# Per-token factors spread over channels by transposes, and values transposed two chunks at a time

## The chip, the cores and the metric

One Trainium2 chip, one of its cores. The metric is device microseconds of one execution of the whole program, as the median of runs on the chip. Beside the runs stands one profiled execution, whose trace is read below.

## The reference

One inference step of a one-layer hybrid decoder: 512 prompt tokens and 8 x 8 sampled tokens, 576 in all, with 1024 channels. Cut to what matters here:

```python
u = rmsnorm(h, norm_mix)                       # h * rsqrt(mean(h*h) + eps) * g, per token
proj = u @ w_in                                # z, xbc, dt, rw
# group A: SSD (Mamba-2) with conv, silu, gate, and a grouped RMSNorm of the output
yg = yg * lax.rsqrt(jnp.mean(yg * yg, axis=-1, keepdims=True) + NORM_EPS)   # 2 groups of 512 channels
# group B: RWKV-7, 16 heads of 64 channels
kk = heads(k * k_k)
kk = kk / jnp.maximum(jnp.sqrt(jnp.sum(kk * kk, axis=-1, keepdims=True)), 1e-12)   # per token and head
s = s * w - (s @ kk) (kk * a)^T + v k^T        # per token; evaluated here in chunks of 64 tokens
o = s @ r
on = (o - mean(o)) * lax.rsqrt(var(o) + GN_EPS) * ln_x_w + ln_x_b           # per token and head
out = concat(y_ssd, (on + bonus) * gate) @ w_out
h += out; h += SwiGLU(rmsnorm(h)); h += sigmoid(rmsnorm(h) @ w_plg) * (p @ w_plp); y = rmsnorm(h)
```

Four kinds of factor belong to a token (or to a token and a head) and are applied to all its channels: the row norms, the group norm of group A, the norm of `kk`, and the deviation of `o`.

## The kernel before, in words

Activations are kept with channels on the 128 partitions and the 576 tokens along the free dimension (64 sampled tokens first, then 512 of the prompt). A linear layer multiplies f32 data as high and low parts, three matmuls of 128x128 by 128x288 each (`mm3`, L210 to L212), into a tile of the pool `lin`: two tiles of two PSUM banks each, used in turn by all projections, by the low-rank products (`lora`), the gate products and the bonus sums (`fsum`, L225). The other four banks are `cx` (two), `tr` (one) and `cb` (one).

Group B runs in four quarters of four heads, that is two channel tiles (`jj`) each. For a quarter, `prep` makes the decays, keys and norms, `gram` the products between tokens of a chunk, `solve` and `combine` invert the triangular blocks (VectorE, with round trips through DRAM; L638 and L640 are its inner loop), `chain` walks through the 9 chunks of 64 tokens (chunk 0 is the sampled tokens), and `head_norm` normalises the output. Projections that are not needed yet are put in between (`fill`). The program text gives priorities; a planner in the framework puts the instructions of each engine in order ahead of time, from its own costs, so parts of different quarters are interleaved finely on every engine. Semaphores and the reuse of tiles follow from that order. `head_norm` of the last quarter has a raised priority.

A factor per token is made with the tokens on the partitions and must come back to channels on the partitions. Tokens are cut in five windows of 128, `WIN`; 576 is four and a half times 128, so the fifth overlaps the fourth by 64.

- `token_sums` (L469) adds up squares over the channels of a head: matmuls whose output has tokens on partitions.
- `inv_norm` takes the square root (ScalarE) and the reciprocal (VectorE).
- `by_channel` copies the factor to 64 columns a head (L486, or L490 and L492) and multiplies each window by the identity, as a plain f32 product (L495), into one PSUM bank of 512 tokens; the last 64 tokens go by a product over 64 partitions (L498) into a second bank. It hands the two pieces back one after the other, and VectorE multiplies each into `kk` (L548, bank `cb`) or into the output (L877, banks `cx`).
- `rstd_by_token` does the same for the factors of a whole token (sums L306, products L313). It is called for the first norm, twice for the group norm of group A, for the two norms around the feed-forward part, and for the two halves of the final norm.

In `chain`, the values `v` of a chunk are needed with tokens on partitions, in the tile `suv(g)`, where each of the two heads of a channel tile sits on its own half of the partitions. `vwin(w)` transposes 128 tokens from token 64 w on (two transposes, L722, into `tr`), and `vput` copies from it with ScalarE: one half to chunk w + 1 for the first head, the other to chunk w for the second head. The first chunk's and the last chunk's other heads come from small 64x64 products with the identity (`edge`, L811 and L812), the last one by way of the tile `vl`. So each chunk is preceded by a window of its own:

```python
        for g in range(1, 9):
            if g < 8:
                w = vwin(g)
                vput(g + 1, 0, w)
                vput(g, 1, w)
```

`bktok` transposes the keys of a chunk (L730, also into `tr`), and `core`, `prompt_state` and `outp` are the products of the chunk.

Of the kernel before, what the change touches and what calls it, by code (L numbers as in the profile page):

```python
# [74 lines left out]
def hybrid_step(ctx, tc, A):  # L75
# [31 lines left out]
    WIN = ((0, 0, 128), (1, 128, 128), (2, 256, 128), (3, 384, 128), (4, 448, 128))  # L107
# [140 lines left out]
    def tr_ps():  # L248
        return bank(sq_, "tr", 1)
# [49 lines left out]
    def rstd_by_token(acc, scale, a=0, b=NT, banks=None):  # L299

        t = None if banks else lin_bank()
        n = (b - a) // P
        ws = [(a + i * P, 0) for i in range(n)] + [(b - P, 64)] * ((b - a) % P // 64)
        st = banks[1][:, 96:96 + len(ws)] if banks else t[:, 600:600 + len(ws)]
        for i, (c, _) in enumerate(ws):
            T.matmul(st[:, i:i + 1], acc[:, c:c + P], ones[:, 0:1], start=True, stop=True)  # L306
        rn = cp.tile([P, 5], F32, tag="rn5", name=nm("rn5"), bufs=2)
        act(rn[:, 0:len(ws)], st, AF.Sqrt, scale=scale, bias=eps_t[:, 0:1])
        V.reciprocal(rn[:, 0:len(ws)], rn[:, 0:len(ws)])
        for i, (c, p) in enumerate(ws):  # L310
            o = c + p - a
            o = banks[o // 512][:, o % 512:o % 512 + P - p] if banks else t[:, o:o + P - p]
            T.matmul(o, rn[p:P, i:i + 1].to_broadcast([P - p, P]), ident[p:P, p:P],  # L313
                     start=True, stop=True)
        return None if banks else t[:, 0:b - a]
# [3 lines left out]
    act(r0[:, 0:512], banks[0][:])  # L319
    act(r0[:, 512:NT], banks[1][:, 0:64])  # L320
# [145 lines left out]
    def token_sums(st, jj, sq):  # L466

        for w, a, n in WIN:
            T.matmul(st[:, w * 4 + jj * 2:w * 4 + jj * 2 + 2], sq[:, a:a + n], blk[:, 0:P:64], start=True, stop=True)  # L469
# [11 lines left out]
    def by_channel(rn, jj, psum, tag):  # L481

        rnv = rn[:].rearrange("p (w h) -> p w h", w=5)[:, :, jj * 2:jj * 2 + 2].unsqueeze(3)
        if tag:
            rx = sp.tile([P, 5, 2, 64], F32, tag=tag, name=nm(tag), bufs=1)
            V.tensor_copy(rx[:], rnv.to_broadcast([P, 5, 2, 64]))  # L486
            rx4 = rx[:, 4]
        else:
            rx = slot("rx", [P, 4, 2, 64])
            V.tensor_copy(rx[:], rnv[:, 0:4].to_broadcast([P, 4, 2, 64]))  # L490
            rx4 = s2.tile([P, 2, 64], F32, tag="rx4", name=nm("rx4"))
            V.tensor_copy(rx4[:], rnv[:, 4].to_broadcast([P, 2, 64]))  # L492
        ps = psum()
        for w, a, n in WIN[:4]:
            T.matmul(ps[:, a:a + n], rx[:, w].rearrange("p a b -> p (a b)"), ident[:], start=True, stop=True)  # L495
        yield 0, 512, ps[:, 0:512]
        ps = psum()
        T.matmul(ps[:, 0:64], rx4[64:128].rearrange("p a b -> p (a b)"), ident[64:128, 64:128], start=True, stop=True)  # L498
        yield 512, NT, ps[:, 0:64]

    def prep(s):
# [26 lines left out]
        for jj in jj2:  # L528
# [18 lines left out]
            for a0, b0, ps in by_channel(rn, jj, cb_ps, ""):  # L547
                V.scalar_tensor_tensor(kk[:, a0:b0], k[:, a0:b0], par("k_k", j), ps, ALU.mult, ALU.mult)  # L548
# [155 lines left out]
    def chain(s):  # L704
# [9 lines left out]
        def vput(g, e, ps):  # L714
            h = H[1 - e]
            src = ps[h].rearrange("p (j c) -> p j c", j=2)[:, :, e * 64:e * 64 + 64]
            act(suv(g)[h, :, :, e], src.unsqueeze(2).to_broadcast([64, 2, 2, 64]))

        def vwin(w):
            ps = tr_ps()  # L720
            for jj in jj2:
                T.transpose(ps[:, jj * P:(jj + 1) * P], vv[jj][:, w * 64:w * 64 + 128], ident[:])  # L722
            return ps[:, 0:256]
# [85 lines left out]
        edge = tr_ps()  # L809
        for jj in jj2:  # L810
            T.matmul(edge[H[1], jj * P:jj * P + 64], vv[jj][H[0], 0:64], ident[H[0], 0:64], start=True, stop=True)  # L811
            T.matmul(edge[H[0], jj * P + 64:jj * P + 128], vv[jj][H[1], 512:576], ident[H[1], 64:128],  # L812
                     start=True, stop=True)
        vlast = sp.tile([64, 2, 64], F32, tag="vl", name=nm("vl"))
        act(vlast[:], edge[0:64, 0:256].rearrange("p (j c) -> p j c", j=2)[:, :, 64:128])
        for e in range(2):
            G.memset(suv(1)[H[e], :, 0, e], 0.0)
        vput(0, 0, edge[:, 0:256])
        w = vwin(0)
        vput(1, 0, w)  # L820
        vput(0, 1, w)
        for e in range(2):
            G.tensor_copy(suv(0)[H[e], :, 0, e], ident[H[e], H[e]].unsqueeze(1).to_broadcast([64, 2, 64]))
        for g in range(1, 9):
            if g < 8:
                w = vwin(g)
                vput(g + 1, 0, w)
                vput(g, 1, w)
            else:
                act(suv(8)[0:64, :, :, 1], vlast[:].unsqueeze(2).to_broadcast([64, 2, 2, 64]))  # L830
            bktok(g)
            core(g)
            prompt_state(g)
# [19 lines left out]
    def head_norm(s, ahead=()):  # L853
# [18 lines left out]
        for jj in jj2:  # L872
# [3 lines left out]
            for a, b, ps in by_channel(rn, jj, cx_ps, "rxg"):  # L876
                V.scalar_tensor_tensor(o[:, a:b], o[:, a:b], par("ln_x_w", j), ps, ALU.mult, ALU.mult)  # L877
# [80 lines left out]
    def ssd():  # L958
# [193 lines left out]
        def gated(g):  # L1152
# [18 lines left out]
            act(std[:, 0:512], banks[0][:])  # L1171
            act(std[:, 512:NT], banks[1][:, 0:64])
# [314 lines left out]
```

## Time and profile before

| | |
|---|---|
| Median of 3 runs | 1425.92 us (1424.22 to 1428.69) |
| Profiled execution | 1428.9 us, span 1427.1 us |
| Mean granted TensorE clock in it | 0.944 |
| Busy: TensorE / VectorE / ScalarE / GpSimd | 1318.6 / 726.2 / 584.3 / 548.9 us |
| TensorE matmul records | 10007 |
| DMA | 135.48 MB, mean 95 GB/s |

In the rows of the profile, PE is TensorE's matmul, PEld its weight load, DVE VectorE, ACT ScalarE, POOL GpSimd, SP the queue that issues DMAs. A group's row gives line, engine, operation, output tile <- input tiles, shapes and count, then busy time in us and the mean duration in ns, then the idle time of the engine just before and what ended it. A row of the time order gives start, length (first start to last end of the merged instructions), engine and instruction; matmuls overlap, so the distance between starts tells how long TensorE is held. A row of the chain gives start, the length that the chain spends there, and the place. A row of the waits gives who waited for whom, the us in total, how often, and the longest.

From about 900 us on, the span is the feed-forward part and what follows it, with TensorE busy almost without a gap; before that, the four quarters (to about 725 us) and group A's scan (to about 870 us) share the engines.

### The profile page before, as it was taken

The page shows a single profiled execution, that of the slowest core. Times are in us where ns is not written, and L with a number is a line of the kernel's source. Part 1 is how long each engine was busy: PE and PEld are TensorE (multiplying, and loading weights), DVE is VectorE, ACT ScalarE, POOL GpSimd, SP SyncE. Part 2 cuts the span into 40 slices and gives each one's busy share as a digit, 9 for nine tenths or more (in the row PEclk, how much of TensorE's full clock was granted, in tenths as well). Part 3 has the DMA queues.
Part 4 walks back from the last instruction along what each step waited for, and adds up shares of the span by engine and source line. Part 5 has one row for each costly group of instructions (what it writes and reads, how often), then busy time and mean ns, then how long its engine had stood idle before and what let it go on. Part 6 is the DMA issues. An engine that isn't in the chain of part 4 may idle for free.

```text
span 1427.1 us, 25249 instructions
## 1 busy us (share of the span) xinstructions
PE 1318.6 (92%) x10007; PEld 1215.1 (85%) x10007; DVE 726.2 (51%) x1338; ACT 584.3 (41%) x1185; POOL 548.9 (38%) x545
## 2 busy tenths in 40 slices
PE   6897999999989988979889998999999999999996
PEld 6786897798779967957766787999999999999986
DVE  6548768696767657854365564522222122122264
ACT  6564436543653355434422254433232332222252
POOL 5344515622434235214354454522232332344432
PEclk9998999999989989969959999999999999999998
DMA  4322233233223312343513541322322222223421
GB/s 155 126 60 75 72 107 107 60 89 109 63 86 87 101 56 86 114 135 116 181 61 127 167 123 45 90 74 84 86 82 82 82 82 82 84 83 82 146 80 67
DMA packets 94453, 135.48 MB, mean 95 GB/s; under 512 B 34704, under 2 KB 39056, under 8 KB 94336
## 3 DMA queue, kind: packets, MB, share of 16 engines
q1 hardware_dynamic: 94336, 133.88, 30.7%
q8 instruction: 78, 1.28, 0.4%
q14 instruction: 39, 0.32, 0.1%
HBM read 106.10 MB, written 27.75 MB: 94 GB/s over the span
## 4 chain that ended last, share of the span: by engine, by line
PE 67%; DVE 18%; ACT 4%; DMA 4%; issue 3%; POOL 1%; SPq 1%; DVEq 0%; ACTq 0%; POOLq 0%
PE lin L210 17%; PE lin L212 17%; PE lin L211 17%; DVE Tt L640 2%; DVE tmp L638 2%; PE lin L580 2%; DVE h L369 2%; PE d L1116 1%; PE y L1147 1%; DVE wlo L195 1%; PE y L1149 1%; DMA L<-Ld 1%; DMA raw<-wts 1%; PE cx L802 1%; DVE suv L785 1%
## 5 line engine op out<-in xcount | busy, mean ns | idle before, releaser
L210 PE MATMUL lin<-xhi,whi 128*128 128x288 f32 (+1 forms) x1488 | 450.8, 303 | 4.5 <-ACT xhi L92 1.9
L212 PE MATMUL lin<-xhi,wlo 128*128 128x288 f32 (+1 forms) x1488 | 449.9, 302 | 3.3 <-DVE wlo L195 1.9
L211 PE MATMUL lin<-xlo,whi 128*128 128x288 f32 (+1 forms) x1488 | 449.2, 302 | 0.6 <-POOL xlo L183 0.6
L195 POOL TENSOR_TENSOR wlo<-raw,whi 128x512 fp32r<-128x512 f32 x137 | 180.6, 1319 | 467.0 <-ACT whi L92 452.6
L92 ACT ACTIVATE whi<-raw 128x512 fp32r<-128x512 f32 (+1 forms) x272 | 169.0, 621 | 403.1 <-PE lin L211 330.6
L210 PEld LDWEIGHTS lin<-xhi,whi 128*128 128x128 f32 (+1 forms) x1488 | 283.7, 191 | 13.3 <-issue 5.1
L212 PEld LDWEIGHTS lin<-xhi,wlo 128*128 128x128 f32 (+1 forms) x1488 | 284.7, 191 | 9.0 <-DVE wlo L195 3.2
L211 PEld LDWEIGHTS lin<-xlo,whi 128*128 128x128 f32 (+1 forms) x1488 | 283.9, 191 | 5.7 <-issue 3.5
L195 DVE TENSOR_TENSOR wlo<-raw,whi 128x512 fp32r<-128x512 f32 (+1 forms) x135 | 96.8, 717 | 157.7 <-ACT whi L92 157.4
L212 PE MATMUL lin<-ah,wlo 128*128 128x288 f32 x352 | 104.0, 295 | 0.4
L210 PE MATMUL lin<-ah,whi 128*128 128x288 f32 x352 | 104.1, 296 | 0.0
L211 PE MATMUL lin<-al,whi 128*128 128x288 f32 x352 | 103.8, 295 | 0.0
L212 PEld LDWEIGHTS lin<-ah,wlo 128*128 128x128 f32 x352 | 66.3, 188 | 1.3 <-POOL wlo L195 1.3
L211 PEld LDWEIGHTS lin<-al,whi 128*128 128x128 f32 x352 | 66.1, 188 | 0.0
L210 PEld LDWEIGHTS lin<-ah,whi 128*128 128x128 f32 x352 | 66.0, 187 | 0.0
L1294 DVE TENSOR_TENSOR sg<-lin,sg 128x576 f32<-128x576 f32 x22 | 16.7, 758 | 79.6 <-PE lin L212 78.3
L1289 DVE TENSOR_TENSOR sg<-lin,rstd 128x576 f32<-128x576 f32 x22 | 16.7, 758 | 72.9 <-PE lin L212 71.9
L640 DVE TENSOR_TENSOR Tt<-Tt,tmp 72x30 f32<-72x30 f32 (+14 forms) x120 | 48.8, 407 | 3.3
L638 DVE TENSOR_TENSOR tmp<-L,Tt 72x30 f32<-72x30 f32 (+14 forms) x120 | 47.1, 392 | 3.2
L210 PE MATMUL lin<-xu,whi 128*128 128x288 f32 x128 | 40.0, 314 | 8.9 <-ACT xu L92 7.5
L212 PE MATMUL lin<-xu,wlo 128*128 128x288 f32 x128 | 39.9, 313 | 6.0 <-DVE wlo L195 5.4
L211 PE MATMUL lin<-y,whi 128*128 128x288 f32 x128 | 39.2, 306 | 4.2 <-DVE y L183 4.0
(372 smaller groups left out, 2657.5 us busy)
## 6 DMA issues: line engine op xcount, KB each, us to landing
raw<-wts SPq DMA_DIRECT2D x271, 256.0 KB, 2.7
S<-s_wkv SPq DMA_DIRECT2D x8, 512.0 KB
hd<-s_ssm SPq DMA_DIRECT2D x8, 512.0 KB
o_ssm_s<-hd SPq DMA_DIRECT2D x8, 512.0 KB
xbc_d<-E SPq DMA_DIRECT2D x12, 288.0 KB, 2.4
x<-xT SPq DMA_DIRECT2D x8, 288.0 KB, 6.1
gate_d<-g SPq DMA_DIRECT2D x8, 288.0 KB, 2.8
bv_d<-bv SPq DMA_DIRECT2D x8, 288.0 KB, 2.1
```

What stands on the lines that cost most here:

```text
L92: S.activation(out, in_, func, bias=bias, scale=scale)
L195: eng.tensor_tensor(lo[:, 0:n], raw[:, 0:n], hi[:, 0:n].bitcast(F32), ALU.subtract)
L210: T.matmul(ps[:, a:b], whi, xhi[:, a:b], start=first, stop=False)
L211: T.matmul(ps[:, a:b], whi, xlo[:, a:b], start=False, stop=False)
L212: T.matmul(ps[:, a:b], wlo, xhi[:, a:b], start=False, stop=last)
L369: V.scalar_tensor_tensor(h[:], E[:, i:i + 600], w(i), h[:], ALU.mult, ALU.add)
L580: T.matmul(ps[:, c:c + 256], s.BK[jj][:, g].rearrange("p a t -> p (a t)"), s.G[:, g, jj].rearrange("p a e t -> p (a e t)"), start=True, st ...
L638: V.tensor_tensor(o, L[:, jx:jx + 1, jx + 1:32].to_broadcast([NB, jx, n]), Tt[:, 0:jx, jx:jx + 1].to_broadcast([NB, jx, n]), ALU.mult)
L640: V.tensor_tensor(Tt[:, 0:jx, jx + 1:32], Tt[:, 0:jx, jx + 1:32], o, ALU.subtract)
L785: V.scalar_tensor_tensor(dst, sv[h, jj, 0, e], PC[h, jj, 7 + g:8 + g], dw[h, jj, e], ALU.mult, ALU.add)
L1289: V.tensor_tensor(s_[:], ps, rs[:], ALU.mult)
L1294: V.tensor_tensor(s_[:], up, s_[:], ALU.mult)
```

## The change

Per-token factors are spread by TensorE transposes of 128x128 instead of products with the identity. `WIN` becomes five starting points, all 128 wide; the fourth window begins at 320, so that no window crosses a PSUM bank when the output starts 64 columns into a two-bank tile. `by_channel` takes a tile of `lin` instead of two banks of `cb` or `cx`, and hands back one piece of 576 tokens, for which VectorE needs one instruction. `rstd_by_token` transposes in the same way; where it is given two banks, the first takes 448 tokens and the second 128. In `chain`, one pair of transposes serves two chunks (windows at tokens 0, 128, 256, 384 and 448), both heads are copied from it, and the edge products go. The window for the next two chunks is put between `core(g)` and `prompt_state(g)` of an odd chunk g; the one for chunks 2 and 3 ahead of chunk 2.

```diff
@@ -104,7 +104,7 @@
         return pool.tile([P, 512], F32, tag=tag, name=nm(tag), bufs=bufs)
 
     HV = ((0, HALF), (HALF, NT))
-    WIN = ((0, 0, 128), (1, 128, 128), (2, 256, 128), (3, 384, 128), (4, 448, 128))
+    WIN = (0, 128, 256, 320, 448)
 
 
     def const(name, shape, dt=F32):
@@ -299,25 +299,23 @@
     def rstd_by_token(acc, scale, a=0, b=NT, banks=None):
 
         t = None if banks else lin_bank()
-        n = (b - a) // P
-        ws = [(a + i * P, 0) for i in range(n)] + [(b - P, 64)] * ((b - a) % P // 64)
-        st = banks[1][:, 96:96 + len(ws)] if banks else t[:, 600:600 + len(ws)]
-        for i, (c, _) in enumerate(ws):
+        ws = WIN if b - a == NT else [min(c, b - P) for c in range(a, b, P)]
+        off = 64 if b - a == NT else -a
+        st = banks[1][:, 200:200 + len(ws)] if banks else t[:, 700:700 + len(ws)]
+        for i, c in enumerate(ws):
             T.matmul(st[:, i:i + 1], acc[:, c:c + P], ones[:, 0:1], start=True, stop=True)
         rn = cp.tile([P, 5], F32, tag="rn5", name=nm("rn5"), bufs=2)
         act(rn[:, 0:len(ws)], st, AF.Sqrt, scale=scale, bias=eps_t[:, 0:1])
         V.reciprocal(rn[:, 0:len(ws)], rn[:, 0:len(ws)])
-        for i, (c, p) in enumerate(ws):
-            o = c + p - a
-            o = banks[o // 512][:, o % 512:o % 512 + P - p] if banks else t[:, o:o + P - p]
-            T.matmul(o, rn[p:P, i:i + 1].to_broadcast([P - p, P]), ident[p:P, p:P],
-                     start=True, stop=True)
-        return None if banks else t[:, 0:b - a]
+        for i, c in enumerate(ws):
+            o = banks[c // 448][:, c % 448:c % 448 + P] if banks else t[:, c + off:c + off + P]
+            T.transpose(o, rn[:, i:i + 1].to_broadcast([P, P]), ident[:])
+        return None if banks else t[:, a + off:b + off]
 
     banks = cx_ps(), cx_ps()
     rstd_by_token(accs[V], 1.0 / D, banks=banks)
-    act(r0[:, 0:512], banks[0][:])
-    act(r0[:, 512:NT], banks[1][:, 0:64])
+    act(r0[:, 0:448], banks[0][:, 0:448])
+    act(r0[:, 448:NT], banks[1][:, 0:128])
 
     X = []
 
@@ -465,8 +463,8 @@
 
     def token_sums(st, jj, sq):
 
-        for w, a, n in WIN:
-            T.matmul(st[:, w * 4 + jj * 2:w * 4 + jj * 2 + 2], sq[:, a:a + n], blk[:, 0:P:64], start=True, stop=True)
+        for w, a in enumerate(WIN):
+            T.matmul(st[:, w * 4 + jj * 2:w * 4 + jj * 2 + 2], sq[:, a:a + P], blk[:, 0:P:64], start=True, stop=True)
 
     def inv_norm(st, tag, scale, eps):
         rn = sp.tile([P, 20], F32, tag=tag, name=nm(tag), bufs=2)
@@ -478,7 +476,7 @@
         V.reciprocal(rn[:], rn[:])
         return rn
 
-    def by_channel(rn, jj, psum, tag):
+    def by_channel(rn, jj, tag):
 
         rnv = rn[:].rearrange("p (w h) -> p w h", w=5)[:, :, jj * 2:jj * 2 + 2].unsqueeze(3)
         if tag:
@@ -490,13 +488,11 @@
             V.tensor_copy(rx[:], rnv[:, 0:4].to_broadcast([P, 4, 2, 64]))
             rx4 = s2.tile([P, 2, 64], F32, tag="rx4", name=nm("rx4"))
             V.tensor_copy(rx4[:], rnv[:, 4].to_broadcast([P, 2, 64]))
-        ps = psum()
-        for w, a, n in WIN[:4]:
-            T.matmul(ps[:, a:a + n], rx[:, w].rearrange("p a b -> p (a b)"), ident[:], start=True, stop=True)
-        yield 0, 512, ps[:, 0:512]
-        ps = psum()
-        T.matmul(ps[:, 0:64], rx4[64:128].rearrange("p a b -> p (a b)"), ident[64:128, 64:128], start=True, stop=True)
-        yield 512, NT, ps[:, 0:64]
+        t = lin_bank()
+        for w, a in enumerate(WIN):
+            by = rx[:, w] if w < 4 else rx4
+            T.transpose(t[:, 64 + a:64 + a + P], by.rearrange("p a b -> p (a b)"), ident[:])
+        return t[:, 64:64 + NT]
 
     def prep(s):
         q = s.q
@@ -544,8 +540,7 @@
             G.memset(pb[:, 0:65:8], 1.0)
             G.memset(pb[:, 128:NT:64], 1.0)
             kk = slot("kk")
-            for a0, b0, ps in by_channel(rn, jj, cb_ps, ""):
-                V.scalar_tensor_tensor(kk[:, a0:b0], k[:, a0:b0], par("k_k", j), ps, ALU.mult, ALU.mult)
+            V.scalar_tensor_tensor(kk[:], k[:], par("k_k", j), by_channel(rn, jj, ""), ALU.mult, ALU.mult)
             bk = (se, sp)[q % 2].tile([P, 9, 2, 64], F32, tag=f"bk{q % 2}", name=nm("bk"), bufs=2)
             V.tensor_tensor(pb[:, 0:NT], kk[:], pb[:, 0:NT], ALU.mult)
             for e in range(2):
@@ -711,16 +706,20 @@
                 SUV[g] = sp.tile([P, 2, 2, 2, 64], F32, tag="suv", name=nm("suv"), bufs=3)
             return SUV[g]
 
-        def vput(g, e, ps):
-            h = H[1 - e]
-            src = ps[h].rearrange("p (j c) -> p j c", j=2)[:, :, e * 64:e * 64 + 64]
-            act(suv(g)[h, :, :, e], src.unsqueeze(2).to_broadcast([64, 2, 2, 64]))
-
-        def vwin(w):
+        def vput(g, ps, half):
+            src = ps[half].rearrange("p (j c) -> p j c", j=2)
+            for e in range(2):
+                act(suv(g)[H[1 - e], :, :, e],
+                    src[:, :, e * 64:e * 64 + 64].unsqueeze(2).to_broadcast([64, 2, 2, 64]))
+
+        def vwin(g):
+
             ps = tr_ps()
+            a = min(g, 7) * 64
             for jj in jj2:
-                T.transpose(ps[:, jj * P:(jj + 1) * P], vv[jj][:, w * 64:w * 64 + 128], ident[:])
-            return ps[:, 0:256]
+                T.transpose(ps[:, jj * P:(jj + 1) * P], vv[jj][:, a:a + 128], ident[:])
+            for i in range(g, min(g + 2, 9)):
+                vput(i, ps[:, 0:256], H[i - min(g, 7)])
 
         bkt = {}
 
@@ -806,30 +805,18 @@
                                 ALU.mult)
             nc.sync.dma_start(A["o_wkv_s"][q], S0[:])
 
-        edge = tr_ps()
-        for jj in jj2:
-            T.matmul(edge[H[1], jj * P:jj * P + 64], vv[jj][H[0], 0:64], ident[H[0], 0:64], start=True, stop=True)
-            T.matmul(edge[H[0], jj * P + 64:jj * P + 128], vv[jj][H[1], 512:576], ident[H[1], 64:128],
-                     start=True, stop=True)
-        vlast = sp.tile([64, 2, 64], F32, tag="vl", name=nm("vl"))
-        act(vlast[:], edge[0:64, 0:256].rearrange("p (j c) -> p j c", j=2)[:, :, 64:128])
         for e in range(2):
             G.memset(suv(1)[H[e], :, 0, e], 0.0)
-        vput(0, 0, edge[:, 0:256])
-        w = vwin(0)
-        vput(1, 0, w)
-        vput(0, 1, w)
+        vwin(0)
         for e in range(2):
             G.tensor_copy(suv(0)[H[e], :, 0, e], ident[H[e], H[e]].unsqueeze(1).to_broadcast([64, 2, 64]))
         for g in range(1, 9):
-            if g < 8:
-                w = vwin(g)
-                vput(g + 1, 0, w)
-                vput(g, 1, w)
-            else:
-                act(suv(8)[0:64, :, :, 1], vlast[:].unsqueeze(2).to_broadcast([64, 2, 2, 64]))
+            if g == 2:
+                vwin(g)
             bktok(g)
             core(g)
+            if g % 2 and 1 < g < 8:
+                vwin(g + 1)
             prompt_state(g)
             outp(g)
             if g == 1:
@@ -873,8 +860,7 @@
             j = 2 * q + jj
             o = Oc[jj]
             gt, y = ahead[jj]
-            for a, b, ps in by_channel(rn, jj, cx_ps, "rxg"):
-                V.scalar_tensor_tensor(o[:, a:b], o[:, a:b], par("ln_x_w", j), ps, ALU.mult, ALU.mult)
+            V.scalar_tensor_tensor(o, o, par("ln_x_w", j), by_channel(rn, jj, "rxg"), ALU.mult, ALU.mult)
             (V if q == 3 else G).tensor_tensor(y, y, o, ALU.add)
             yo = sp.tile([P, NT], F32, tag="gt", name=nm("yo"), bufs=2)[:] if q == 2 and jj else y
             V.scalar_tensor_tensor(yo, y, par("ln_x_b", j), gt, ALU.add, ALU.mult)
@@ -1168,8 +1154,8 @@
             std = mt("bc", [P, NT], bufs=4)
             banks = d_ps(), d_ps()
             rstd_by_token(qa, 1.0 / 512, banks=banks)
-            act(std[:, 0:512], banks[0][:])
-            act(std[:, 512:NT], banks[1][:, 0:64])
+            act(std[:, 0:448], banks[0][:, 0:448])
+            act(std[:, 448:NT], banks[1][:, 0:128])
             for i in range(4):
                 j = 4 * g + i
                 V.scalar_tensor_tensor(xs[j][:], xs[j][:], par("ssd_norm", j), std[:], ALU.mult, ALU.mult)
```

## The prediction

> **What bounds the kernel now.** I began with the page: the engines' busy time, then the chain of work that ended last.
>
> ```profile
> span 1427.1 us, 25249 instructions
> PE 1318.6 (92%) x10007; PEld 1215.1 (85%) x10007; DVE 726.2 (51%) x1338; ACT 584.3 (41%) x1185; POOL 548.9 (38%) x545
> PEclk9998999999989989969959999999999999999998
> PE 67%; DVE 18%; ACT 4%; DMA 4%; issue 3%; POOL 1%; SPq 1%; DVEq 0%; ACTq 0%; POOLq 0%
> ```
>
> TensorE is the resource: busy 92% of the span and 67% of the chain. An instruction taken off TensorE is worth something where the chain runs through it, so the next view was the chain in order of time, searched for the lines that the change touches.
>
> ```profile
> 28.26 0.91 PE cx L313 x8
> 95.90 1.64 PE cb L495 x7
> ...
> 224.48 0.37 PE tr L722 x2
> 224.85 0.89 PE cb L495 x8
> 227.59 0.36 PE cb L498 x2
> ...
> 343.21 0.36 PE cx L498 x2
> ...
> 716.84 2.09 PE cx L495 x8
> ...
> 836.15 1.25 PE d L313 x10
> 867.26 1.17 PE d L313 x8
> 937.31 1.25 PE lin L313 x10
> 1418.67 1.24 PE lin L313 x4
> ```
>
> Columns are start, length on the chain, engine, tile, line. L495 is the four full identity products of one spreading by channel, L498 its half product, L313 the same for the row norms, L722 the value transposes. The list of longest pieces has twelve pieces of L495 (first and last shown), 13.5 us together, out of sixteen calls: three quarters of these products lie on the path. The eight records at 716.84 take 2.09 us against 0.89 at 224.85, because there the clock is low (the PEclk row has a 5 in that slice).
>
> **What one product and one transpose cost.** First the groups, kept apart by shape.
>
> ```profile
> L722 PE MATMUL tr<-ident,rw 128*128 128x128 f32 x64 | 14.5, 308 | 3.1 <-ACT suv L92 2.3 <-ACT bkt L92 0.7
> L495 PE MATMUL cx<-ident,rxg 128*128 128x128 f32 x64 | 12.3, 355 | 3.2 <-DVE rxg L486 3.2
> L495 PE MATMUL cb<-ident,rx 128*128 128x128 f32 x64 | 9.6, 294 | 1.6 <-DVE rx L490 1.6
> L498 PE MATMUL cx<-ident,rxg 64*128 64x64 f32 x16 | 4.5, 371 | 0.0
> L498 PE MATMUL cb<-ident,rx 64*128 64x64 f32 x16 | 3.5, 296 | 0.2 <-DVE kk L548 0.2
> L811 PE MATMUL tr<-ident,rw 64*64 64x64 f32 x16 | 2.2, 257 | 0.4 <-ACT gnr L92 0.4
> ```
>
> The counts say it: 16 calls of 4 products make 64 products but 128 records, so a product of two f32 operands runs as two matmuls; the 32 pairs of L722 make 64 records, so a transpose runs as one. The mean durations are alike, since neighbours overlap; what counts is the distance from start to start.
>
> ```profile
> 220.07 0.38 PE L730 MATMUL tr<-ident,bk 128*128 128x128 f32 x2
> 220.21 0.38 PE L212 MATMUL lin<-ulh,wlo 128*128 128x288 f32 x1
> ...
> 224.68 1.06 PE L495 MATMUL cb<-ident,rx 128*128 128x128 f32 x8
> 225.50 0.38 PE L210 MATMUL lin<-xhi,whi 128*128 128x288 f32 x1
> ...
> 343.14 0.43 PE L498 MATMUL cx<-ident,rxg 64*128 64x64 f32 x2
> 343.50 0.40 PE L211 MATMUL lin<-xlo,whi 128*128 128x288 f32 x1
> ```
>
> Eight product records hold TensorE for 0.82 us (224.68 to 225.50), the half product for 0.36 us, together 1.18 us a call. Two transposes of the same size (L730, the keys) hold it for 0.14 us, and run as 0.38 us = 0.27 + 0.11, so each further one adds 0.11: five come to 0.14 + 3 x 0.11 = 0.47, with some change of operand type to either side (a pair of L722 has 0.37 on the chain at 224.48) say 0.60 us.
>
> The Trainium skill ("TensorE: Matmul & The Clock Gate", section "Terms") says that the weight load's and matmul's transpose mode is four times faster for FP32. By the rows above it is two matmuls against one of the same pitch, a factor of two; with a factor of four each of the 150 new transposes would take some 0.05 us less, and with half of that on the path the sum would be 4 us lower, an estimate.
>
> **The change part by part.**
>
> (a) Spreading by channel, 16 calls (two channel tiles in each of four quarters, in the preparation and in the head norm). 160 records become 80. Warm, a call saves 1.18 - 0.60 = 0.58 us; four of the sixteen calls, the last quarter's two and the two before them, lie in a stretch with the low clock, at twice that. 12 x 0.58 + 4 x 1.16 = 11.6 us of TensorE, three quarters of it on the path: **-8.7 us**. All of it on the path is the one end, a third of it the other.
>
> (b) VectorE's second, 64-wide multiply after each spreading goes; the 512-wide one becomes 576 wide.
>
> ```profile
> L877 DVE SCALAR_TENSOR_TENSOR ar<-ar,pv,cx x16: 273/508/750, 343.2 to 723.5; 128x512 f32<-128x512 f32 x8, 128x64 f32<-128x64 f32 x8
> L548 DVE SCALAR_TENSOR_TENSOR kk<-rw,pv,cb 128x512 f32<-128x512 f32 x8 | 6.0, 748 | 4.4 <-PE cb L495 4.3
> DVE kk L548 <- PE cb L498: 6.3, 5, 3.3
> DVE ar L877 <- PE cx L495: 8.8, 7, 2.5
> ```
>
> The shortest L877, 0.27 us, is the 64-wide one: 16 x 0.27 = 4.3 us of VectorE, less a few hundredths each for the wider one. VectorE also stood idle 6.3 us for the half product, which could start only when its one bank was read. VectorE is 18% of the chain: **-1 us**, with 0 and -4.3 as ends.
>
> (c) The row norms, seven calls, 30 products (60 records) to 30 transposes. They are serial: sums, square root, reciprocal, spreading, copy. The five chain rows of L313 add up to 5.8 us; half of the records go: **-3 us**, with -2 and -4 as ends, since the list leaves out short pieces. The copies behind them are the same two instructions, cut at 448 instead of 512: nothing, and at worst the same work again.
>
> (d) Values: 32 pairs of transposes become 20, the 16 edge products of 64x64 go. A pair costs 0.14 to 0.37 us: 12 x 0.25 = 3 us; the edge products run side by side (L811's 2.2 us of busy time covers its twin L812) and give 2 us. Half of the 5 us on the path: **-2.5 us**, ends 0 and -5. ScalarE loses one small copy a quarter, costed at nothing, since ScalarE is 41% busy; without that cover it would be another 1 us of gain.
>
> What moves on ScalarE: four value copies now come in a row after every second chunk, where two came before each chunk.
>
> ```profile
> L92 ACT ACTIVATE suv<-tr 64x256 f32<-64x256 f32 x68 | 25.7, 377 | 24.9 <-PE tr L722 11.6 <-DVE suv L785 8.0 <-POOL um L800 4.6
> ```
>
> The next chunk's copies of the key transposes and of xs stand behind them in ScalarE's queue, and the solve step's small products wait for xs. Two more copies ahead are 0.75 us; in 16 places 12 us if every one is exposed. Against it, ScalarE idled 11.6 us for L722's transposes, and there will be 20 such places instead of 32. I take zero, with +12 and -5 as ends.
>
> (e) The spreading by channel now takes a tile of the `lin` pair, the double buffer of the projections, instead of the `cb` or `cx` banks. That is the added wait: a projection whose tile is still held has to stand, and the whole of TensorE's queue behind it. The nearest rows are the short users that `lin` already has: 16 low-rank products, 8 bonus sums, 8 gate products.
>
> ```profile
> PE lin L210 <- DVE bv L565: 2.5, 2, 2.0
> PE lin L210 <- ACT lo L92: 1.2, 1, 1.2
> PE lin L210 <- ACT g L92: 0.6, 2, 0.5
> ```
>
> 4.3 us over 32 uses is 0.13 us a use; sixteen more: **+2 us**. The lower end is zero; the upper comes under the rivals.
>
> **Sum.** -8.7 - 1 - 3 - 2.5 + 2 = -13.2 us. The profiled execution took 1428.9 us (span 1427.1 and 1.8 around it), 3.0 above the median 1425.92. Taken from the median: 1412.7, so **1413 us**, 0.9% faster. A change under 0.3% (4.3 us) I call none, since the three runs spread over that much.
>
> **Rivals.**
>
> *The gain is hidden* (no change). Without TensorE's work the chain goes through the triangular solve on VectorE and its round trips through DRAM instead; only (c) and about 1 us of the last head norm, after which nothing else is left to run, remain: 1422. For it: VectorE is 18% of the chain. Against it: twelve of sixteen calls of L495 lie on the chain now.
>
> *The whole of TensorE's work counts* (faster). 11.6 + 4 + 5 and 4.3 of VectorE: 25 us, 1401 us. For it: TensorE is the only engine near full. Against it: the 33% of the chain that is elsewhere.
>
> *The double buffer* (slower). Each spreading holds one of the two `lin` tiles until VectorE gets to its multiply, which has a queue of its own.
>
> ```profile
> 246.84 1.05 PE L495 MATMUL cb<-ident,rx 128*128 128x128 f32 x8
> ...
> 248.99 0.75 DVE L548 SCALAR_TENSOR_TENSOR kk<-rw,pv,cb 128x512 f32<-128x512 f32 x1
> ```
>
> Here the bank is held from 246.84 to 249.74, 2.9 us, of which 2.1 after the products. If each of the 16 calls made the next projection wait as long, that is 34 us: 1425.9 - 15.2 + 34 = 1445. It decides at 15.2 / 16 = 0.95 us a call. For it: only two tiles, and the projection before is often still being read by ScalarE and VectorE. Against it: a projection runs for several us, longer than 2.9, and the 32 short users of today wait little.
>
> *The clock* (no change, or slower). Row by row:
>
> ```profile
> 600.00:650.00 50.00, 8.71 (x41) 6.47 (x41) 4.32 (x12) 0.69 0.52 160
> 650.00:700.00 50.00, 4.46 (x22) 2.55 (x22) 6.02 (x16) 1.00 0.37 125
> ```
>
> The third figure from the right is the granted clock; the rows count the instructions on the transposes' bank. A mean of 0.69 over 50 us means about 31 us at half rate, which costs 15 us of full-rate work. One more such stretch would eat the gain: 1428. The Trainium skill ("TensorE: Matmul & The Clock Gate", section "Part 4: PE-mode transpose") says that transposes do not count as TensorE activity for the clock gate. By that rule more transposes mean more low clock; the trace disagrees as far as it goes, for the stretch from 650 to 700 us, with 22 transposes in it, has the full clock.
>
> **How the numbers follow.** Forecast 0.50, whole of TensorE 0.12, hidden 0.15, double buffer 0.16, clock 0.07. The forecast's own range is 1402 to 1421: (a) from all of the path to a third of it, and (b), (d) and (e) at their ends. ScalarE's queue could add its 12 us to the forecast, 1425; and since the planner puts the instructions of all engines in an order worked out from its own costs, that order will differ everywhere, by an amount that no row bounds. The range for 8 in 10 is 1400 to 1434: it takes in the whole-TensorE case, the hidden case, ScalarE's queue and the lower half of the double buffer's. Faster: 0.50 + 0.12 and a little of the hidden case, 0.64; same: most of the hidden case and half of the clock's, 0.17; slower: 0.19.
>
> **What the changed profile would show.** TensorE records down by 80 + 30 + 24 + 32 = 166, to 9841, and its busy time down by 15 to 30 us. Five records a call at 0.47 to 0.65 us start to next in place of L495 and L498. VectorE with 16 instructions fewer. The last head norm's spreading at about 1.1 us instead of 2.09. If (e) is wrong, the list of waits shows a projection's first matmul waiting for the multiply of the spreading, above 0.13 us a call. If ScalarE's queue is the trouble, xs waits for a value copy and TensorE's waits on xs grow. If the chain moved, its share on VectorE rises above 18% and the span falls less than TensorE's busy time. What would make it wrong without any of these: a planner's order with longer idle stretches, seen as lower clock around 600 to 750 us.

## The result and the profile after

The changed kernel took 1633.82 us, the median of 4 runs (1628.85 to 1634.18), against 1425.37 us: a ratio of 1.1437, 95% interval 1.1403 to 1.147. It is 208 us slower, where 1413 us was forecast. The ratios in this text are worked out from all undisturbed runs of both sides (one run of `no_lin` below, 5973 us at a granted clock of 0.185, is left out), so they need not be the quotient of two medians.

The page of the profiled execution, the parts that answer to those of before (totals, granted clock by slice, the chain by engine):

```profile
span 1632.4 us, 24965 instructions
PE 1352.4 (83%) x9841; PEld 1226.7 (75%) x9841; DVE 707.0 (43%) x1322; ACT 594.9 (36%) x1185; POOL 549.6 (34%) x545
PEclk9987588985979957897979699989999999999998
PE 65%; DVE 18%; ACT 7%; DMA 4%; issue 3%; POOL 1%; SPq 1%; DVEq 0%; ACTq 0%; POOLq 0%
```

The instructions that were to go are gone: 9841 records on TensorE, 16 instructions fewer on VectorE. Yet TensorE idles for 280 us (1632.4 - 1352.4) where it idled for 108.5, and its busy time rose although it does less. Where the idle time lies, the longest wait of TensorE says (who <- whom: us in total, times, longest), in the kernel after, then in the kernel before:

```profile
PE cx L657 <- DMA AA<-Ad: 99.0, 8, 30.0
PE tr L729 <- POOL bk L609: 14.1, 6, 3.8
PE lin L494 <- DVE rx L488: 12.9, 4, 4.6
PE lin L494 <- DVE rxg L484: 9.5, 6, 1.6
```

```profile
PE cx L662 <- DMA AA<-Ad: 1.5, 2, 0.9
```

AA is the result of the triangular solve, read back from DRAM by `combine`. TensorE now stands for up to 30 us at a time until the solve of VectorE is through. Busy times by stretch of the kernel after (start and end of the stretch, its length, busy us of PE, PEld, DVE, ACT and POOL with counts, granted clock, DMA share, GB/s): the first quarter's gram, its solve, its chunk chain, its head norm, the second quarter's preparation, gram and solve:

```profile
131.00:153.00 22.00, 14.42 (x46) 10.28 (x46) 9.01 (x17) 8.86 (x21) 16.87 (x25) 0.73 0.24 57
153.00:183.00 30.00, 0.31 (x2) 0.17 (x2) 21.64 (x63) 0.00 (x0) 0.30 (x1) 0.50 0.15 30
188.00:235.00 47.00, 37.55 (x298) 27.38 (x293) 15.20 (x49) 16.59 (x54) 7.10 (x10) 0.81 0.14 48
237.00:255.00 18.00, 13.82 (x62) 12.15 (x63) 6.83 (x11) 3.20 (x6) 6.11 (x4) 0.62 0.06 20
256.00:340.00 84.00, 74.12 (x545) 70.31 (x545) 41.42 (x66) 46.09 (x82) 23.13 (x32) 0.98 0.27 79
345.00:366.00 21.00, 12.37 (x49) 8.22 (x48) 9.96 (x18) 9.04 (x23) 19.85 (x25) 0.91 0.27 71
366.00:395.00 29.00, 0.00 (x0) 0.00 (x0) 21.81 (x63) 0.42 (x2) 0.48 (x1) 0.50 0.11 25
```

The same view of the kernel before, for the first quarter's solve and its chunk chain:

```profile
157.00:197.00 40.00, 38.45 (x286) 36.38 (x283) 35.90 (x87) 15.97 (x33) 9.27 (x10) 1.00 0.28 87
210.00:317.00 107.00, 99.48 (x761) 86.96 (x760) 85.60 (x165) 58.39 (x137) 48.53 (x69) 0.97 0.30 87
```

Before, the solve ran beside 38.45 us of TensorE work: projections that are needed later. After, it runs beside 0.31 us, on an engine whose clock has gone to half (0.50). And the chunk chain of the first quarter, 107 us long before because the whole preparation of the second quarter was woven into it, is 47 us long and runs alone. The instructions that write or read a `lin` tile show what went missing (PE, PEld, DVE, ACT, then as above), in that solve and that chain, in the kernel before and then after:

```profile
157.00:197.00 40.00, 38.11 (x276) 35.37 (x273) 3.70 (x8) 4.70 (x14) 1.00 0.28 87
210.00:317.00 107.00, 72.01 (x438) 62.38 (x439) 7.50 (x16) 14.22 (x37) 0.97 0.30 87
```

```profile
153.00:183.00 30.00, 0.00 (x0) 0.00 (x0) 0.00 (x0) 0.00 (x0) 0.50 0.15 30
188.00:235.00 47.00, 0.00 (x0) 0.00 (x0) 0.00 (x0) 0.00 (x0) 0.81 0.14 48
```

Nearly all of the work beside the solve was work on `lin`, and after the change not one instruction touches `lin` from the end of the gram to the head norm. The gram products (L580 before, L575 after; PE and PEld alone) date it exactly: how many of them run in the first gram, in the first chain, in the second gram as before, in the first head norm; then the kernel after, with its second gram in the last row.

```profile
137.00:157.00 20.00, 9.63 (x36) 7.85 (x36) 0.92 0.29 73
210.00:317.00 107.00, 9.53 (x36) 7.02 (x36) 0.97 0.30 87
264.00:285.00 21.00, 9.53 (x36) 6.68 (x35) 0.94 0.27 66
320.00:353.00 33.00, 0.00 (x0) 0.00 (x0) 0.90 0.38 103
```

```profile
131.00:153.00 22.00, 10.19 (x36) 8.21 (x36) 0.73 0.24 57
188.00:235.00 47.00, 0.00 (x0) 0.00 (x0) 0.81 0.14 48
237.00:255.00 18.00, 0.00 (x0) 0.00 (x0) 0.62 0.06 20
345.00:366.00 21.00, 8.84 (x36) 6.51 (x36) 0.91 0.27 71
```

Before, the second quarter's gram falls inside the first quarter's chain (264 to 285, in 210 to 317), and its solve starts there. After, it comes 90 us behind the first head norm. The overlap of the quarters is lost: each quarter runs preparation, gram, solve, chain, head norm, one after the other.

### The profile page after: what moved, and what is told of

The parts are those of the page before. It is cut to its first block, busy times and chain, and to the rows that moved or that the text cites. A ratio compares the mean times of both kernels' runs of the same rounds, so it can differ in the third digit from the quotient of the medians.

```text
span 1632.4 us, 24965 instructions
## 1 busy us (share of the span) xinstructions
PE 1352.4 (83%) x9841; PEld 1226.7 (75%) x9841; DVE 707.0 (43%) x1322; ACT 594.9 (36%) x1185; POOL 549.6 (34%) x545
## 4 chain that ended last, share of the span: by engine, by line
PE 65%; DVE 18%; ACT 7%; DMA 4%; issue 3%; POOL 1%; SPq 1%; DVEq 0%; ACTq 0%; POOLq 0%
PE lin L210 16%; PE lin L212 16%; PE lin L211 16%; DVE Tt L635 3%; DVE tmp L633 2%; ACT suv L92 2%; PE cx L753 1%; PE cx L776 1%; DVE suv L784 1%; DVE h L367 1%; PE d L1102 1%; PE lin L494 1%; PE y L1133 1%; PE cx L853 1%; PE lin L575 1%
## 5 line engine op out<-in xcount | busy, mean ns | idle before, releaser
L657 PE MATMUL cx<-AA,Lst 32*32 32x32 f32 x256 | 8.9, 237 | 99.0 <-DMA AA<-Ad 99.0
L657 PEld LDWEIGHTS cx<-AA,Lst 32*32 32x32 f32 x256 | 7.8, 150 | 101.0 <-DMA AA<-Ad 101.0
L799 POOL TENSOR_TENSOR um<-suv,dmb 128x512 f32<-128x512 f32 x16 | 16.4, 1043 | 138.3 <-ACT suv L92 134.9
L1280 DVE TENSOR_TENSOR sg<-lin,sg 128x576 f32<-128x576 f32 x22 | 16.7, 758 | 79.6 <-PE lin L212 78.3
L1275 DVE TENSOR_TENSOR sg<-lin,rstd 128x576 f32<-128x576 f32 x22 | 16.7, 757 | 71.8 <-PE lin L212 71.6
L575 PE MATMUL lin<-G,bk 128*128 128x256 f32 x144 | 38.3, 418 | 10.0 <-ACT G L92 5.5
```

The lines of the kernel that those rows point to most:

```text
L575: T.matmul(ps[:, c:c + 256], s.BK[jj][:, g].rearrange("p a t -> p (a t)"), s.G[:, g, jj].rearrange("p a e t -> p (a e t)"), start=True, st ...
L657: T.matmul(Wv[hi_:hi_ + 32, g - 1, jj, :], s.Lst[lo_:lo_ + 32, g, jj, 32:64], AA[lo_:lo_ + 32, g, jj, :], start=True, stop=True)
L799: G.tensor_tensor(um[:], sv[:, jj, 1, e].unsqueeze(1).to_broadcast([P, 8, 64]), dmb[:].unsqueeze(2).to_broadcast([P, 8, 64]), ALU.mult)
L1275: V.tensor_tensor(s_[:], ps, rs[:], ALU.mult)
L1280: V.tensor_tensor(s_[:], up, s_[:], ALU.mult)
```

## The experiments

The edits are shown cut to the lines that matter, against the changed kernel, or against the kernel before where the name or the text says so; where a bank is chosen, `by_channel` gets it as an argument again.

Three theories were put to the test. Theory 1: the head norm's spreading takes its tile from `lin`; tiles of a pool are handed out in the order of the program text, so all `lin` tiles of the next quarter, which stand behind it in the text, must come behind it in time. Theory 2: the double-buffer rival of the prediction, a price for each use, because a tile is held while VectorE is late. Theory 3: the paired values and ScalarE's queue.

**Head norm back in its own banks** (`hn_cx`).

```diff
-  V.scalar_tensor_tensor(o, o, par("ln_x_w", j), by_channel(rn, jj, "rxg"), ALU.mult, ALU.mult)
+  for a0, b0, ps in by_channel(rn, jj, cx_ps, "rxg"):   # transposes: 448 tokens, then 128
+      V.scalar_tensor_tensor(o[:, a0:b0], o[:, a0:b0], par("ln_x_w", j), ps, ALU.mult, ALU.mult)
```

> The changed kernel, but the head norm's spreading uses the two cx banks again (transposes: 448 tokens into one, 128 into the next, two multiplies); the preparation's spreading stays in lin. Theory 1 (order of tiles): the head norm's lin tile stands, in program order, ahead of all lin tiles of the next quarter's preparation and gram, so these cannot run during the chain before it; with cx the quarters overlap again: the gram of the second quarter starts before the first head norm, TensorE's wait for AA at the combine falls from 99 us to under 20, and the time is 1405 to 1425 us, as first forecast. Theory 2 (a held tile): each spreading holds one of two lin tiles while VectorE is late, in either place; half of the calls remain, so about half of the loss of 208 us: 1500 to 1550. Theory 3 (the paired values, ScalarE's queue): no change, 1620 to 1640.

Measured: 1415.88 us, ratio 0.9915 (0.9888 to 0.9943). The whole loss is gone. The paired values are still in it, so theory 3 is out. That the first forecast's 1413 is within 3 us is luck in part: its terms, measured one by one below, are off in both directions. Its totals, its wait for AA, and its gram products (L585) in the first gram, the first chain, the second gram and the first head norm:

```profile
PE 1299.6 (92%) x9841; PEld 1196.1 (85%) x9841; DVE 719.9 (51%) x1330; ACT 584.6 (41%) x1181; POOL 557.3 (39%) x545
PE cx L667 <- DMA AA<-Ad: 0.2, 1, 0.2
core 0: 1414.9 us, clock 0.940
...
131.00:153.00 22.00, 10.15 (x36) 8.18 (x36) 0.87 0.27 69
205.00:311.00 106.00, 8.64 (x36) 6.52 (x36) 0.94 0.29 88
257.00:278.00 21.00, 8.64 (x36) 6.52 (x36) 1.00 0.24 63
313.00:348.00 35.00, 0.00 (x0) 0.00 (x0) 0.85 0.38 104
```

The second gram is inside the first chain again. Against this kernel, with the same 9841 records, the changed kernel's 217.5 us of span split in two: 1352.4 - 1299.6 = 52.8 us more busy time, and the rest, 164.7 us, more idle time of TensorE. How much of the 52.8 us is the lower clock can be estimated from the two traces: with the busy time of each stretch of 2 us weighted by its granted clock, the sums are 1249 and 1234 us, so some 38 us are the clock and the other 15 us are not accounted for.

**Preparation back in its own bank, head norm left in `lin`** (`prep_cb`).

```diff
-  V.scalar_tensor_tensor(kk[:], k[:], par("k_k", j), by_channel(rn, jj, ""), ALU.mult, ALU.mult)
+  for a0, b0, ps in by_channel(rn, jj, cb_ps, ""):
+      V.scalar_tensor_tensor(kk[:, a0:b0], k[:, a0:b0], par("k_k", j), ps, ALU.mult, ALU.mult)
```

> The changed kernel, but the preparation's spreading uses the cb bank again (transposes, two multiplies); the head norm's stays in lin. Theory 1: the preparation's lin tiles stand among other lin tiles of the same preparation, so moving them changes little: 1600 to 1640, TensorE's wait for AA still 80 us or more. Theory 2: half of the loss goes, 1500 to 1550. Theory 3: 1620 to 1640, so this run tells theory 1 from 2 only.

Measured: 1648.38 us, ratio 1.1527 (1.146 to 1.1595), slightly above theory 1's range and nowhere near theory 2's half. TensorE's wait for AA is 95.3 us. Eight of the sixteen uses of `lin` went and nothing was won.

**The kernel before, with only the head norm's products moved to `lin`** (`before_hn_lin`).

```diff
-  ps = psum()
+  t = lin_bank(); ps = t[:, 0:512]          # head norm only
   ...                                       # the four products, L495
-  ps = psum()
+  ps = t[:, 512:576]
   ...                                       # the half product, L498
```

> The kernel before, with one edit: the head norm's identity products go into one lin tile instead of two cx banks. No transposes, no paired values, the same number of instructions. Theory 1: this edit alone makes the loss: 1600 to 1660, with the second quarter's gram after the first head norm and TensorE's wait for AA at 80 us or more. Theory 2: eight calls hold a lin tile, half of the loss at most: 1500 to 1550. Theory 3: as before, 1425.

Measured: 1677.54 us, ratio 1.175 (1.1698 to 1.1803), above theory 1's range. There is not one transpose more in it than before. The tile alone makes the loss, some 250 us; the transposes and the rest of the change take 44 us of it back. Its gram (L581) in the first gram, the first chain, the first head norm, and behind:

```profile
137.00:158.00 21.00, 9.69 (x36) 7.85 (x36) 0.74 0.23 58
192.00:242.00 50.00, 0.00 (x0) 0.00 (x0) 0.74 0.14 46
244.00:269.00 25.00, 0.00 (x0) 0.00 (x0) 0.61 0.04 15
370.00:390.00 20.00, 9.25 (x36) 7.49 (x36) 0.76 0.24 61
```

**The changed kernel with the head norm later in the text** (`hn_later`).

```diff
   prep(s); start_states(s); gram(s); decayed(s)
+  if s.q:
+      head_norm(Q[s.q - 1])
   if s.q < 3:
       inverse(s); chain(s)
-      head_norm(s)
```

> The changed kernel with its lin tiles kept in both places, but the program text has the head norm of a quarter after the preparation, gram and decay of the next quarter instead of before them. Theory 1: the next quarter's lin tiles now come first, its preparation and gram can run during the chain again; most of the loss goes: 1410 to 1480, and the second quarter's gram starts before the first head norm. Theory 2: the same calls hold the same tiles: 1600 or more. Theory 3: 1600 or more.

Measured: 1439.84 us, ratio 1.0081 (1.0054 to 1.0109). All sixteen spreadings still use `lin`; only the text's order differs, and 194 of the 208 us come back. Its gram (L575) in the first gram, the first chain, the second gram and the first head norm, and its wait for AA:

```profile
131.00:153.00 22.00, 9.10 (x36) 7.18 (x36) 0.93 0.27 69
205.00:287.00 82.00, 8.63 (x36) 6.52 (x36) 0.90 0.27 80
256.00:276.00 20.00, 8.63 (x36) 6.52 (x36) 0.95 0.34 91
289.00:311.00 22.00, 0.00 (x0) 0.00 (x0) 0.56 0.05 18
...
PE cx L657 <- DMA AA<-Ad: 5.1, 4, 1.9
```

**One small tile is enough** (`st_lin`): the fast variant with the head norm's 20 columns of sums put into a `lin` tile.

```diff
-  st = tr_ps()[:, 0:20]
+  st = lin_bank()[:, 0:20]
```

> The fast variant (head norm's spreading in cx, 1415.9) with one line changed: the 20 columns of the head norm's sums by token go into a tile of lin instead of the tr bank, one use a quarter instead of two, and no spreading in it. Theory 1 (order of tiles): that one small tile per head norm is enough to keep the next quarter's lin tiles behind it: 1580 to 1650, TensorE's wait for AA and for the solve comes back, and the second quarter's gram begins after the first head norm. Theory 2 (a held tile, price by use): four uses in place of sixteen, 1416 to 1450.

Measured: 1607.1 us, ratio 1.1252 (1.1221 to 1.1284), 191 us above the variant without that line. Its gram (L585) in the same four places as for `before_hn_lin`, and its wait for AA:

```profile
131.00:153.00 22.00, 10.19 (x36) 8.21 (x36) 0.73 0.23 57
187.00:234.00 47.00, 0.00 (x0) 0.00 (x0) 0.81 0.14 48
236.00:263.00 27.00, 0.00 (x0) 0.00 (x0) 0.94 0.18 55
337.00:359.00 22.00, 8.60 (x36) 6.51 (x36) 0.91 0.30 79
...
PE cx L667 <- DMA AA<-Ad: 99.2, 8, 30.2
```

Four uses of `lin` in the head norms, in place of eight there, cost nearly as much (the preparation's eight are in both): theory 2, a price for each use, is out as the cause of the loss, and the place of the head norm's transposes and multiplies has nothing to do with it.

This run also says what kind of order it is. The head norm takes one of the two tiles here. The other one is idle all through the solve and the chain (no instruction touches `lin` from 153 to 234 us). These are the head norm's first sums, the first projection after them, and the head norm's last sums:

```profile
238.10 0.61 PE L467 MATMUL lin<-blk,gsq 128*128 128x2 f32 x4 [0.51 <-ACT gsq L92]
238.93 0.79 PE L210 MATMUL lin<-xhi,whi 128*128 128x288 f32 x1
...
244.48 0.50 PE L467 MATMUL lin<-blk,gsq 128*128 128x2 f32 x4
```

The projection starts 0.8 us after the head norm's first product, while the head norm's tile is still being filled. So it did not wait for a held tile to come free; it stood behind the head norm's first use of the pool.

**The preparation's side of the sharing, with products** (`before_prep_lin`).

```diff
-  ps = psum()
+  t = lin_bank(); ps = t[:, 0:512]          # preparation only; the half product into t[:, 512:576]
```

> The kernel before with one edit: the preparation's identity products go into one lin tile instead of two turns of the cb bank; still products, still two multiplies. Theory 1: these tiles stand among lin tiles of the same preparation and no overlap is lost: 1420 to 1432; at the first forecast's price of 0.13 us a use, +1 us. If the single cb bank was a brake (VectorE idled 6.3 us for the half product), it is faster by about that: 1418 to 1423. If holding a lin tile costs 1 us a use or more: over 1434.

Measured: 1429.88 us, ratio 1.0017 (1.0001 to 1.0033): +2.4 us for eight uses (0.1 to 4.7). The same tile, eight times as well, at another place of the text: 2 us against 250. The single `cb` bank was no brake either: with it gone VectorE idles 16.7 us for the half product, 6.3 us before, and the kernel is not faster.

**What the parts are worth when the overlap is kept.** Four variants: all transposes but no spreading in `lin` (`no_lin`); the paired values alone (`vals_only`); the row norms alone (`rstd_only`); the spreading alone, with `lin` in the preparation and `cx` in the head norm (`spread_only`).

```diff
 # no_lin:      by_channel(rn, jj, cb_ps, "") in the preparation, by_channel(rn, jj, cx_ps, "rxg") in the head norm
 # vals_only:   before + vput, vwin and the loop over g of the changed kernel
 # rstd_only:   before + rstd_by_token of the changed kernel and the copies at 448
 # spread_only: before + by_channel and WIN as in hn_cx
```

> All transposes and paired values, no spreading in lin: the preparation's goes to the one cb bank in two pieces, the head norm's to the two cx banks. If a use of lin in the preparation costs the 0.13 us a use that the first forecast took, this is within 4 us of the run with the preparation in lin (1415.9): 1411 to 1420. If the preparation's lin tiles are worth more than they cost (one multiply, no wait for the single cb bank), it is slower than that run, 1420 to 1430; if they hold up the projections, it is faster, under 1411.

Measured: 1425.05 us, ratio 0.9975 (0.9953 to 0.9997). With the preparation in `lin` it is 0.9915; in this version of the kernel `lin` in the preparation is worth some 9 us, where it was worth nothing with products (`before_prep_lin`).

> The kernel before with the paired value transposes alone. First forecast's term: -2.5 us, 1422 to 1425 with before at 1426. If four value copies in a row on ScalarE delay the chunk chain: 1430 to 1438.

Measured: 1425.86 us, ratio 0.9989 (0.9972 to 1.0007). No effect that can be told from none: the interval runs from -4.0 to +1.0 us. The branch of harm, 1430 us or more, is excluded; the gain of 2.5 us is not decided.

> The kernel before with transposes in the row norms alone (rstd_by_token and its copies). First forecast's term: -3 us, 1422 to 1424. If a transpose is no shorter than a product in a serial stretch: 1426.

Measured: 1432.73 us, ratio 1.0023 (1.0002 to 1.0044): a loss of 3 us (0.3 to 6.3) where a gain of 3 was expected, although the calls are shorter (the first takes 0.71 us, 1.42 before).

> The kernel before with the spreading by channel alone done by transposes, in lin in the preparation and in the cx banks in the head norm; row norms and values as before. First forecast's terms for it: -8.7 - 1 + 2 = -7.7 us, less half of the multiply's gain: 1418 to 1420. If the gain lies elsewhere: 1424 or more. The three terms measured alone should add up to the run with all of them (-10 us) if they are independent; if the planner's order decides, they will not add up.

Measured: 1410.36 us, ratio 0.9875 (0.9856 to 0.9893): -18 us, more than twice the forecast terms, and the fastest kernel of the study, in front of both given kernels.

**Do the terms add up?** (`spread_vals`: the spreading as above and the paired values.)

```diff
 # spread_only + vput, vwin and the loop over g of the changed kernel
```

> The kernel before with the spreading by transposes (lin in the preparation, cx in the head norm) and the paired values; row norms as before. If the terms add up: 1410.4 from the spreading alone and 1 to 3 us off for the values, 1407 to 1410. If the planner's order decides, anywhere from 1405 to 1425, and the run with the row norms too (1415.9) is no sign that these cost time.

Measured: 1416.2 us, ratio 0.9928 (0.9907 to 0.995). Adding the values to the spreading costs 6 us; adding the row norms to that (`hn_cx`) costs nothing more, where alone they cost 3. The parts do not add up; the differences are 5 to 10 us either way. A planner's order that differs from kernel to kernel would explain it, but no run isolates that, and which order is good for what reason was not settled.

## Why the prediction was wrong

The step that failed is (e). It said what the added wait was, "a projection whose tile is still held has to stand", and priced it at 0.13 us a use, +2 us in all, from 32 short users of `lin`. All of these users stand inside the preparation or the gate products, among the projections whose turn they share. The head norm is not such a place. It stands at the end of a chain of 47 us or more, and a `lin` tile there is a gate between the quarters: nothing behind it in the text that needs `lin`, so no projection and no gram of the next quarter, and with them no solve, started before the chain in front of it had ended. That put 99.0 us of TensorE waiting for the solve where there had been 1.5, and the head norm's eight uses alone cost the kernel before 250 us (`before_hn_lin`), where (e) priced all sixteen at 2 us. The rows could have hinted at it: the kernel before has its second gram at 264 to 285, in the first chain, and neither chain nor head norm uses a `lin` tile there. The question that was missed is not how long a tile is held but what stands behind it in the order of its pool, and what that work was covering.

The double-buffer rival named the right tile and the right sign, but not the mechanism: it reckoned a wait for each call, decided "at 15.2 / 16 = 0.95 us a call" and ended at 1445. In the preparation the price is 2.4 us for eight calls, 0.3 us a call; in the head norm 250 us for eight.

Of the other steps:

- The prices on TensorE held. A spreading in `lin` of the variant `hn_cx`, from its first transpose to the next instruction, takes 0.47 us (start, length, instruction), the lower of the two figures worked out; at a granted clock of 0.50, in the kernel after, it takes 0.98 us:

```profile
243.60 0.71 PE L495 MATMUL lin<-ident,rx 128*128 128x128 f32 x5
244.07 0.38 PE L210 MATMUL lin<-xhi,whi 128*128 128x288 f32 x1
...
249.62 1.33 PE L494 MATMUL lin<-ident,rxg 128*128 128x128 f32 x5 [1.64 <-DVE rxg L484]
250.60 0.59 PE L210 MATMUL lin<-xhi,whi 128*128 128x288 f32 x1
```

- The 166 records went as counted. TensorE's busy time fell by 19.0 us in `hn_cx` (1318.6 to 1299.6), within the 15 to 30 forecast; in the kernel after it rose by 33.8, mostly through the lower clock by the estimate above.
- (a), half of (b) and the preparation's half of (e) are -18 us by `spread_only` against -8.7 - 0.5 + 1 = -8.2. VectorE's wait for the half product, 6.3 us before, went with it, but the prediction's reading that this product could start only when its one bank was read does not explain the surplus: `before_prep_lin` frees the bank, and the wait grows to 16.7 us at an unchanged time. What the surplus is stays open.
- (c) was -3 and measured +3 (+0.3 to +6.3) alone; (d) was -2.5 and measured -1.6 (-4.0 to +1.0) alone. Neither adds up with the rest.
- ScalarE's queue, taken as zero, does no harm of more than 1 us with the values changed alone: `vals_only`.
- The clock rival was right that low clock costs, not on its cause. The mean granted clock went from 0.944 to 0.888, but in `hn_cx`, with the same 150 transposes, it is 0.940. It falls where TensorE idles: 0.50 in the two solves above. The Trainium skill ("TensorE: Matmul & The Clock Gate", section "Part 1: The HAM clock gate (the "warmup" mystery)") has idle windows bring the half rate, and these rows agree. That transposes do not count as activity (section "Part 4" of that page) is not borne out by `hn_cx`; `no_lin`, with the same 150, has 0.931, and what lowers it there stays open.

What stays open is where the order is made. The runs show that it holds, for products, for transposes and for 20 columns of sums, and that it moves with the text. `st_lin` speaks against a wait for a held tile, since the other tile stood idle; that leaves the order that the planner gives TensorE's queue, but no run changes the planner, so this is argued and not shown.

## What to carry to other kernels

Before a buffer is taken from a pool that another stage uses, ask what that pool's next users in program order are, and whether they run ahead today; a small tile at the end of a long dependent chain can fence off a whole stage, whatever its own time is. A short user priced from other short users is priced only for the same place in the program. When an engine is near full, look for the stretches in which another engine leads (here the solve) and note what fills them: that filling is the first thing a new order can lose.

## What the runs showed that was not expected

- One 20-column tile a quarter costs 191 us (1607.1 against 1415.9), 13% of the kernel, with the same 9841 records on TensorE.
- The loss has a second part: 52.8 us of longer busy time for the same 9841 records, of which some 38 us, by the estimate above, is the lower clock of a TensorE that idles.
- With instructions planned ahead of time, small edits have no fixed value: the row norms' shorter transposes measured +3 us alone and the values' 6 us more beside the spreading, so gains under some 10 us had to be measured in the combination that is kept.
